# A bidirectional RWKV layer in fp32: the rate and the gate behind the keys, two products on GpSimd, and the output projection's tiles

## The chip, the cores and the metric

One core of a Trainium2 chip runs the whole kernel. The metric is the device time of one execution in microseconds. Of the engines, TensorE (PE, with its weight loads PEld) multiplies matrices; VectorE (DVE), ScalarE (ACT) and GpSimd (POOL) work on elements; SyncE (SP) issues the DMAs. Each engine takes its instructions in the order of its queue, and semaphores hold an instruction until what it needs is there.

## The reference

A model of three mixers over 512 tokens of 1024 channels with 256 context tokens, all in fp32. Layer 0 is pooling and neighbourhood attention with an MLP, layer 1 the recurrence below with an MLP, and a second block has latent and dilated attention. The change lies in layer 1. Its features, cut to what matters:

```python
mix = lambda j: h + centred_shift(h) * mu[j]
k = mix(2) @ wk;  v = mix(3) @ wv                       # keys, values
kk = heads(k * k_k); kk = kk * rsqrt(sum(kk * kk))      # normalised key
for d in range(2):                                      # both directions
    w_raw = w0[d] + tanh(mix(1) @ w1[d]) @ w2[d]        # decay
    a = sigmoid(a0[d] + (mix(4) @ a1[d]) @ a2[d])       # rate
    k_d = k * (1 + (a - 1) * k_a)
r = mix(0) @ wr
g = sigmoid(mix(5) @ g1) @ g2                           # gate
# for each of 16 heads of 64 channels, per token, forward and backward:
S = S * w - (S @ kk) (x) (kk * a) + v (x) k_d;   y = S @ r
# at the end: ((group_norm(y) * ln_g + ln_b + (r . k_sum . r_k) * v) * g) @ wo
```

## The kernel before

The kernel keeps activations as [128 channels, tokens] tiles, 768 columns for context and tokens together. Dense products are made of three fp32r matmuls: weights and activations are split into a high and a low part (`wsplit` L583/L584, `split_sb` L596/L597), and `mm3` (L590 to L592) adds high times high, low times high and high times low.

The framework gives every engine a fixed queue before the run: a planner simulates the program, and among instructions that could go it takes those first that stand earlier in the program. A dependence can be added by hand without a semaphore: `scan.interleave(work, steps)` spreads a list of matmuls over a list of steps, so that each stands behind its step in PE's queue.

**`features`** (L1325) makes the inputs of the recurrence and stores them in DRAM, in this order: the first halves of decay and rate (`lora`, L1382/L1383); the decay's second half, `lora2("w2bd", ...)` into `sd`; the gate's first half; the rate's second half, `lora2("a2bd", ts[1], hw[:,1], self.td, False)`; `mix(2)`, the keys' input (L1369, L596, L597, eight pieces of 128 channels); the gate's second half `gates(tg)` into `gd`; then `proj(wk, ...)`, which makes the keys in units of 256 channels and calls `evac_k` for each block of 128 (copy L1482, square, key norm with a reciprocal square root at L608, reversal for the backward direction, DMAs into `b0` and `b1`); then the same for receptance (`wr`) and values (`wv`). `lora2` has six matmuls for each of 16 heads, a Tanh evacuation of 512 and of 256 columns (L1405) and a store of 393 KB; `gates` has three matmuls, a copy and a store for each of eight blocks. The evacuated tiles of both, and those of `evac_k`, share three tags of two buffers each.

**The scan** (`Scan`) runs over eight blocks of two heads. `front` loads a head's features, makes the running decay (ACT exponentials), turns the rate into `f0` and `ta` (ACT, L368/L369), multiplies these by the normalised key and the key (`base0`, `base1`: L370/L371, VectorE), makes `bk` (L376/L377), `G` (L387/L390) and the products for the bonus (`prod`, L394/L395), then on PE the products in a chunk (L329) that fill `Ld`. `rest` inverts a 32x32 triangle per chunk: mask on GpSimd (L421), transpose on VectorE (L422), thirty steps of two small operations on GpSimd (`Mt` L427, `M` L428), a memset (L429), transposes on VectorE (L432/L433), copies and matmuls into `T` and `f` (L443 to L471); then twelve steps in order over the chunks (L501 to L512, with `ZU` as the state), the sum `Y` (L520), and the normalisation with gate and bonus (L524 to L547), which stores a row block of `z`. `front` of the next block goes beside `rest` of this one as far as the queues let it.

**`layer1`** (L1251) runs the eight blocks and then multiplies `z` by `wo` (1024 x 1024). The 96 matmuls over row blocks 0 to 5 of `z` (L1290) are issued as `work` beside the last block; the first 48 of them are free and the last 48 are pinned over the 23 steps of that block. Their results go to `yp`; the last two row blocks (`wl`, `z[:, 0]` and `z[:, 1]`, L1308) are multiplied and added once the last block is done. The four `wo` tiles are in slots of the third buffer set of the scan (`hp[2]`, which blocks 2 and 5 use), `zl` has a pool of its own, `wl` is loaded again for the last two.

Of the kernel before, what the change touches and what calls it, by code (L numbers as in the profile page):

```python
# [10 lines left out]
F32 = mybir.dt.float32  # L11
# [4 lines left out]
ALU = mybir.AluOpType  # L16
# [4 lines left out]
NX, NC_, D = 512, 256, 1024  # L21
# [3 lines left out]
CH = 64  # L25
# [207 lines left out]
class Scan:  # L233
# [69 lines left out]
    def front(self, blk):  # L303

        nc = self.nc
# [42 lines left out]
        for hd in range(2):  # L348
            h = blk * 2 + hd

            def load(name, n, src):
                t = fp.tile([128, n], F32, name=name, tag=name)
                nc.sync.dma_start(t, src[h])
                return t

            base0, base1, rd = load("base0", NT, self.p.b0), load("base1", NT, self.p.b1), load("rdup", NX, self.p.rd)

            s, ta = load("sg", NT, self.p.sd), load("ta", NT, self.p.td)
            cs = fp.tile([128, NT], F32, name="cs", tag="cs")
            v3 = lambda t: t.rearrange("p (c t) -> p c t", t=CH)  # L360
            nc.vector.tensor_tensor_scan(cs, self.mreset, s, 0.0, ALU.mult, ALU.add)

            for d in range(2):
                nc.scalar.activation(P[dr[d], d, :, 1:], v3(cs)[dr[d]], AF.Exp, scale=-C0)
                nc.vector.tensor_copy(PC[dr[d], hd, :], P[dr[d], d, :, CH])
            nc.scalar.activation(cs, cs, AF.Exp, scale=C0)
            f0 = fp.tile([128, NT], F32, name="f0", tag="sg")
            nc.scalar.activation(f0, ta, AF.Identity, scale=al[:, 0, h:h + 1], bias=be[:, 0, h:h + 1])  # L368
            nc.scalar.activation(ta, ta, AF.Identity, scale=al[:, 1, h:h + 1], bias=be[:, 1, h:h + 1])  # L369
            nc.vector.tensor_tensor(f0, f0, base0, ALU.mult)  # L370
            nc.vector.tensor_tensor(ta, ta, base1, ALU.mult)  # L371
            bk = []
            for g in range(3):
                t = fp.tile([128, 4, 2, CH], F32, name="bk", tag="bk", bufs=4)
                gs = slice(g * 4, g * 4 + 4)
                nc.vector.tensor_tensor(t[:, :, 0, :], v3(f0)[:, gs], v3(cs)[:, gs], ALU.mult)  # L376
                nc.vector.tensor_tensor(t[:, :, 1, :], v3(ta)[:, gs], v3(cs)[:, gs], ALU.mult)  # L377
                bk.append(t)

            Gs = []
            for g in range(3):
                G = self.hp[blk % 3].tile([128, 8 if g else 4, 4, CH], F32, name="G", tag=f"G{g > 0}", bufs=4 if g else 2)
                gs = slice(g * 256, (g + 1) * 256)
                for d, kk in enumerate((base0, base1)):
                    nc.vector.tensor_tensor(G[:, d], v3(kk[:, gs]), P[:, d, g * 4:(g + 1) * 4, :CH], ALU.mult)  # L387
                if g:
                    r = v3(rd[:, (g - 1) * 256:g * 256]).unsqueeze(1).to_broadcast([128, 2, 4, CH])
                    nc.vector.tensor_tensor(G[:, 2:4], r, P[:, :, g * 4:(g + 1) * 4, 1:], ALU.mult)  # L390
                Gs.append(G)

            pr = fp.tile([128, NX], F32, name="prod", tag="cs")
            nc.vector.tensor_tensor(pr[0:64, :], rd[0:64, :], ta[0:64, NC_:], ALU.mult)  # L394
            nc.vector.tensor_tensor(pr[64:128, :][:, ::-1], rd[64:128, :], f0[64:128, NC_:], ALU.mult)  # L395
            bon = self.p.pt("a")
            vr = slice(hd * 64, hd * 64 + 64)
            nc.tensor.matmul(bon[vr, :], self.p.col("rk", h).to_broadcast([128, 64]), pr, start=True, stop=True)
            nc.scalar.copy(vb[vr, :], bon[vr, :])
            heads.append(Gs)  # L400
            for g in range(4):
                if g < 3:
                    products(g, hd, Gs, bk)
                if g:
                    turn(g - 1, Gs, bk)
# [144 lines left out]
class Prog:  # L550
# [700 lines left out]
    def layer1(self, bcs):  # L1251
        tc, nc = self.tc, self.nc
        dt = lambda n, shape: self.dram.tile(shape, F32, name=n)

        self.b0, self.b1 = dt("b0", [16, 128, NT]), dt("b1", [16, 128, NT])
        self.rd, self.vd = dt("rd", [16, 128, NX]), dt("vd", [D, NX])
        self.vt = dt("vt", [2, NT, D])
        self.zd, self.gd, self.bd = dt("zd", [D, NX]), dt("gd", [D, NX]), dt("bd", [D, NX])

        self.sd, self.td = dt("sd", [16, 128, NT]), dt("td", [16, 128, NT])  # L1260
        xd = dt("xd", [128, 8, NX])
        scan = self.features(self.make_cols(1, self.col("ng", 32, 8), 1, 0, True), bcs, xd)
        scan.late()
        scan.rest()
        for blk in range(1, 7):
            scan.front(blk)
            scan.rest()
        scan.front(7)


        early = 6
        zl = scan.pool("l1z", 1).tile([128, early, NX], F32, name="zl")
        w = [scan.hp[2].tile([128, 8, 4, CH], F32, name="wo", tag="GTrue", bufs=4).rearrange("p a c t -> p (a c t)") for u in range(4)]
        for u in range(4):
            nc.sync.dma_start(w[u], self.i["wo"][u])
        for k in range(early):
            nc.sync.dma_start(zl[:, k, :], self.zd[k * 128:(k + 1) * 128, :])
        scan.drop(scan.fp)
        wop = tc.alloc_tile_pool(name="l1w", bufs=1, side="right")
        z, yp = wop.tile([128, 2, NX], F32, name="z"), wop.tile([128, 8, NX], F32, name="yp")  # L1280
        wl = wop.tile([128, 4, 512], F32, name="wl")
        nc.sync.dma_start(wl, self.i["wo"][:, :, early * 256:].rearrange("u p c -> p u c"))
        scan.rest(z[:, 1, :])
        work = []
        for m in range(8):
            for n in range(2):
                ps, o = self.pt("a"), slice(n * 256, n * 256 + 256)
                for k in range(early):
                    c = k * 256 + m % 2 * 128
                    bi = nc.tensor.matmul(ps[:, :256], w[m // 2][:, c:c + 128], zl[:, k, o], start=k == 0, stop=k == early - 1)  # L1290
                    work.append(bi.ins)
                nc.scalar.copy(yp[:, m, o], ps[:, :256])
        nc.sync.dma_start(z[:, 0, :], self.zd[6 * 128:7 * 128, :])
        scan.interleave(work[48:], scan.steps)
        scan.release("left")
        self.psum(mm=4, s0=1, s1=1, s2=1, b=1)
        self.adatag = "b"
        self.xp = tc.alloc_tile_pool(name="xp", bufs=1)
        self.x = self.xp.tile([128, 8, NX], F32, name="x")
        nc.sync.dma_start(self.x, xd)  # L1300
        y = self.y = self.xp.tile([128, 8, NX], F32, name="y")
        gr = (("x", 0, NX, 0),)
        for g, _, n, o in self.halves(gr):
            for m in range(8):
                ps = self.pt("mm")
                for k in range(2):
                    c = k * 256 + m % 2 * 128
                    nc.tensor.matmul(ps[:, :n], wl[:, m // 2, c:c + 128], z[:, k, o:o + n], start=k == 0, stop=k == 1)  # L1308
                nc.vector.tensor_tensor(y[:, m, o:o + n], ps[:, :n], yp[:, m, o:o + n], ALU.add)
        wop.release()  # L1310
        scan.release("right")
        self.wpools(self.wctx)
        with ExitStack() as ctx:
            E = ctx.enter_context
            self.norms()
            act = E(tc.tile_pool(name="l1act", bufs=1))
            h = self.mid(1, None, y, act, gr)
            self.tap("y1", y)
            self.side = self.ada_vec("ada2", "adab2", self.silu[:, 2:3, :].rearrange("p v k -> p k v"), range(24), self.mod[2])
            bcs = self.mlp(1, h, y, gr)  # L1320
            self.bp.release()
        self.tap("x1", self.x)
        return bcs

    def features(self, A1, bcs, xd):  # L1325
        tc, nc = self.tc, self.nc
# [83 lines left out]
        hw = lp.tile([128, 2, 16], F32, name="hw")  # L1410
# [18 lines left out]
        ts = []  # L1429
        for (_, _, func), ps in zip(both_lora, pss):  # L1430
            t = p2.tile([128, NT], F32, name="lr", tag="rev")
# [7 lines left out]
        nc.scalar.activation(t[:, :NX], ps, AF.Tanh, scale=0.5)  # L1439
        nc.vector.tensor_scalar(t[:, :NX], t[:, :NX], 0.5, 0.5, ALU.mult, ALU.add)  # L1440
        tg = split(t, NX)
        lora2("a2bd", ts[1], hw[:, 1], self.td, False)
        first = lambda j, wname, groups: (self.wsplit(self.i[wname][0]), mix(j, groups))
        wk = first(2, "wk", both)
        gates(tg)

        def rev(src, n, b, fwd, bwd):

# [46 lines left out]
            rev(kk, NT, b, self.b0, self.b1)  # L1495

        proj(wk, "wk", both, evac_k)

        def evac_r(b, pss):
            t = p2.tile([128, NT], F32, name="rblk", tag="kblk")  # L1500
# [456 lines left out]
```

## Time and profile before

| | us |
|---|---|
| median of 3 runs (lowest to highest) | 3165.51 (3158.48 to 3166.71) |
| profiled execution, its own time | 3160.86 |
| span of that execution in the profile | 3158.9 |
| busy in the span: PE, VectorE, ACT, GpSimd | 2820.4, 1789.2, 1551.0, 1140.5 |
| moved by DMA | 346.72 MB, 110 GB/s |

The profile is of one execution, so times of the trace go with 3160.86, not with the median. Times in the trace count from the start of the span. Layer 1's features lie at about 1000 to 1263 us, its scan behind them to about 1990. A group's mean is that of one instruction; for matmuls, which overlap in the engine, the pitch from one to the next is shorter than the duration shown. In a row of groups, the part behind the second bar is the idle time ahead of the group and what ended it.

### The profile page before, as it was taken

How to read it: one execution, taken by the hardware profiler on the slowest of the kernel's cores; microseconds unless marked ns; L12 is line 12 of the kernel's file. 1: busy time of each engine (PE TensorE's matmuls, PEld its weight loads, DVE VectorE, ACT ScalarE, POOL GpSimd, SP SyncE). 2: the span in 40 equal slices, each digit the busy share in tenths (PEclk: the TensorE clock that was granted, in tenths of full speed). 3: DMA queues.
4: the chain of work that ended last, by engine and by line, in shares of the span. 5: the costliest groups of instructions: out<-in, count | busy, mean ns of one | idle time of the engine just before them, and what ended most of it. 6: DMA issues, size and time to landing. Idle time of an engine off the chain costs nothing.

```text
span 3158.9 us, 50961 instructions
## 1 busy us (share of the span) xinstructions
PE 2820.4 (89%) x19290; PEld 2338.0 (74%) x19290; DVE 1789.2 (57%) x3558; ACT 1551.0 (49%) x3103; POOL 1140.5 (36%) x1500
## 2 busy tenths in 40 slices
PE   6999879999996899887777779699997999989999
PEld 6967778888885687764666667587776885678887
DVE  8466383444448725758688742644446654555364
ACT  3247556666664633554566532455543444544341
POOL 4013446667665212045666640256543210010000
PEclk9999989999998999987688889899998995999999
DMA  5323213333331465432233231255441220022322
GB/s 225 125 86 101 101 64 117 127 114 131 118 106 72 187 196 149 167 118 84 81 95 106 83 117 50 99 175 183 169 146 54 81 94 1 15 79 90 104 98 83
DMA packets 138115, 346.72 MB, mean 110 GB/s; under 512 B 16400, under 2 KB 48784, under 8 KB 120592
## 3 DMA queue, kind: packets, MB, share of 16 engines
q1 hardware_dynamic: 137872, 343.48, 31.8%
q8 instruction: 152, 2.49, 0.3%
q14 instruction: 91, 0.75, 0.1%
HBM read 294.40 MB, written 49.02 MB: 109 GB/s over the span
## 4 chain that ended last, share of the span: by engine, by line
PE 32%; DVE 8%; ACT 6%; POOL 6%; DMA 4%; issue 2%; SPq 0%; ACTq 0%; POOLq 0%; DVEq 0%
PE mm L590 7%; PE mm L591 7%; PE mm L592 6%; POOL acc L733 3%; DMA adaw<-in_ada_dram 3%; ACT wh L583 1%; PE st L1247 1%; PE a L329 1%; PE a L1290 1%; POOL M L428 1%; POOL Mt L427 1%; PE y L520 1%; ACT adat L732 1%; PE b L1241 1%; PE a L1924 1%
## 5 line engine op out<-in xcount | busy, mean ns | idle before, releaser
L733 POOL TENSOR_TENSOR acc<-acc,adat 128x256 f32<-128x256 f32 x658 | 575.8, 898 | 529.5 <-ACT acc L729 427.7
L584 DVE TENSOR_TENSOR wl<-wr,wh 128x2048 fp32r<-128x2048 f32 (+3 forms) x145 | 317.7, 2191 | 367.1 <-ACT wh L583 364.6
L732 ACT ACTIVATE adat<-adaw,silu 128x256 f32<-128x256 f32 x644 | 319.1, 508 | 262.1 <-POOL acc L733 161.2
L583 ACT CAST wh<-wr 128x2048 fp32r<-128x2048 f32 (+2 forms) x147 | 266.6, 1814 | 232.0 <-PE mm L591 218.1
L590 PE MATMUL mm<-fh,wh 128*128 128x512 f32 (+1 forms) x1008 | 347.3, 353 | 16.1 <-DVE relu L1015 11.7
L591 PE MATMUL mm<-fl,wh 128*128 128x512 f32 (+1 forms) x1008 | 350.8, 350 | 0.0
L592 PE MATMUL mm<-fh,wl 128*128 128x512 f32 (+1 forms) x1008 | 349.8, 349 | 0.9 <-DVE wl L584 0.9
L590 PE MATMUL mm<-h_xhi,wh 128*128 128x512 f32 (+1 forms) x784 | 278.5, 360 | 3.3 <-ACT h_xhi L596 1.9
L591 PE MATMUL mm<-h_xlo,wh 128*128 128x512 f32 (+1 forms) x784 | 277.9, 357 | 1.8 <-DVE h_xlo L686 1.5
L592 PE MATMUL mm<-h_xhi,wl 128*128 128x512 f32 (+1 forms) x784 | 277.8, 356 | 0.0
L664 POOL TENSOR_TENSOR acc<-acc,t 128x256 f32<-128x256 f32 x127 | 109.0, 866 | 345.5 <-ACT t L662 342.6
L590 PEld LDWEIGHTS mm<-fh,wh 128*128 128x128 f32 x1008 | 190.0, 189 | 43.8 <-DVE relu L1015 14.0
L592 PEld LDWEIGHTS mm<-fh,wl 128*128 128x128 f32 x1008 | 190.6, 189 | 25.5 <-DVE wl L584 1.1
L591 PEld LDWEIGHTS mm<-fl,wh 128*128 128x128 f32 x1008 | 190.7, 189 | 25.3 <-DVE fl L597 2.2
L1039 DVE TENSOR_TENSOR y<-mm,y 128x512 f32<-128x512 f32 (+1 forms) x184 | 99.2, 559 | 141.9 <-PE mm L592 141.4
L590 PE MATMUL mm<-h_hi,wh 128*128 128x512 f32 (+1 forms) x408 | 160.8, 398 | 6.7 <-ACT h_hi L685 6.7
L590 PEld LDWEIGHTS mm<-h_xhi,wh 128*128 128x128 f32 x784 | 148.0, 191 | 23.1 <-ACT h_xhi L596 2.1
L592 PEld LDWEIGHTS mm<-h_xhi,wl 128*128 128x128 f32 x784 | 148.9, 190 | 21.4 <-issue 0.2
L591 PEld LDWEIGHTS mm<-h_xlo,wh 128*128 128x128 f32 x784 | 148.9, 191 | 20.7 <-DVE h_xlo L686 1.7
L427 POOL TENSOR_TENSOR Mt<-M 128x30 f32<-128x30 f32 (+14 forms) x240 | 141.0, 588 | 56.3 <-PE f L443 21.8
L591 PE MATMUL mm<-h_lo,wh 128*128 128x512 f32 (+1 forms) x408 | 160.4, 394 | 0.0
L592 PE MATMUL mm<-h_hi,wl 128*128 128x512 f32 (+1 forms) x408 | 159.5, 393 | 0.0
(451 smaller groups left out, 6932.4 us busy)
## 6 DMA issues: line engine op xcount, KB each, us to landing
adaw<-in_ada_dram SPq DMA_DIRECT2D x256, 256.0 KB, 2.7
wr<-in_w_dram SPq DMA_DIRECT2D x64, 1024.0 KB, 4.9
wr<-in_wup_dram SPq DMA_DIRECT2D x22, 1024.0 KB, 4.8
base<-b SPq DMA_DIRECT2D x32, 384.0 KB, 3.2
ZU<-vt SPq DMA_DIRECT2D x192, 64.0 KB, 2.5
wr<-in_wdn_dram SPq DMA_DIRECT2D x16, 704.0 KB, 4.0
wr<-in_win_dram SPq DMA_DIRECT2D x9, 1024.0 KB, 4.7
wr<-in_evin_dram SPq DMA_DIRECT2D x8, 1024.0 KB, 4.8
```

Source lines behind the costliest of these rows:

```text
L329: nc.tensor.matmul(ps[:, c], bk[g][:, c0 + c].rearrange("p a t -> p (a t)"), G[:, :na, c0 + c, :], start=True, stop=True)
L427: nc.gpsimd.tensor_tensor(t, a, b, ALU.mult)
L428: nc.gpsimd.tensor_tensor(M[:, s + 1:, :s], M[:, s + 1:, :s], t, ALU.add)
L583: nc.scalar.copy(hi[:, :n], raw[:, :n])
L584: (eng or nc.vector).tensor_tensor(lo[:, :n], raw[:, :n], hi[:, :n], ALU.subtract)
L590: mm(out, lhs[0], rhs[0], start=first, stop=False)
L591: mm(out, lhs[0], rhs[1], start=False, stop=False)
L592: return mm(out, lhs[1], rhs[0], start=False, stop=last)
L664: nc.gpsimd.tensor_tensor(acc, acc, sq, ALU.add)
L732: nc.scalar.activation(t, w, AF.Copy, scale=s)
L733: nc.gpsimd.tensor_tensor(acc, acc, t, ALU.add)
L1039: nc.vector.tensor_tensor(yb, ps[:, :n], yb, ALU.add)
```

## The change

`lora2("a2bd", ...)` (the rate's second half) and `gates(tg)` (the gate's) move behind `proj(wk, ...)`, ahead of the receptance. In the scan, the two multiplications L370 and L371 go from VectorE to GpSimd. In `layer1`, the third buffer set is released behind block 5 and the feature pool behind the last `front`; one pool then has all of `z` in eight row blocks, `yp` and the four `wo` tiles, which are each loaded once and whole; the reload `wl` goes; the loads of row blocks 0 to 6 of `z` stand behind `rest(7)` in the program; and all 96 matmuls of `work` are pinned over the 23 steps.

```diff
--- before.py
+++ after.py
@@ -367,8 +367,8 @@
             f0 = fp.tile([128, NT], F32, name="f0", tag="sg")
             nc.scalar.activation(f0, ta, AF.Identity, scale=al[:, 0, h:h + 1], bias=be[:, 0, h:h + 1])
             nc.scalar.activation(ta, ta, AF.Identity, scale=al[:, 1, h:h + 1], bias=be[:, 1, h:h + 1])
-            nc.vector.tensor_tensor(f0, f0, base0, ALU.mult)
-            nc.vector.tensor_tensor(ta, ta, base1, ALU.mult)
+            nc.gpsimd.tensor_tensor(f0, f0, base0, ALU.mult)
+            nc.gpsimd.tensor_tensor(ta, ta, base1, ALU.mult)
             bk = []
             for g in range(3):
                 t = fp.tile([128, 4, 2, CH], F32, name="bk", tag="bk", bufs=4)
@@ -1265,33 +1265,30 @@
         for blk in range(1, 7):
             scan.front(blk)
             scan.rest()
+            if blk == 5:
+                scan.drop(scan.hp[2])
         scan.front(7)
-
-
-        early = 6
-        zl = scan.pool("l1z", 1).tile([128, early, NX], F32, name="zl")
-        w = [scan.hp[2].tile([128, 8, 4, CH], F32, name="wo", tag="GTrue", bufs=4).rearrange("p a c t -> p (a c t)") for u in range(4)]
+        scan.drop(scan.fp)
+
+        wop = tc.alloc_tile_pool(name="l1w", bufs=1, side="right")
+        z, yp = wop.tile([128, 8, NX], F32, name="z"), wop.tile([128, 8, NX], F32, name="yp")
+        w = [wop.tile([128, 2048], F32, name=f"wo{u}") for u in range(4)]
         for u in range(4):
             nc.sync.dma_start(w[u], self.i["wo"][u])
-        for k in range(early):
-            nc.sync.dma_start(zl[:, k, :], self.zd[k * 128:(k + 1) * 128, :])
-        scan.drop(scan.fp)
-        wop = tc.alloc_tile_pool(name="l1w", bufs=1, side="right")
-        z, yp = wop.tile([128, 2, NX], F32, name="z"), wop.tile([128, 8, NX], F32, name="yp")
-        wl = wop.tile([128, 4, 512], F32, name="wl")
-        nc.sync.dma_start(wl, self.i["wo"][:, :, early * 256:].rearrange("u p c -> p u c"))
-        scan.rest(z[:, 1, :])
+        scan.rest(z[:, 7, :])
+        early = 6
+        for k in range(7):
+            nc.sync.dma_start(z[:, k, :], self.zd[k * 128:(k + 1) * 128, :])
+        wcol = lambda m, k: w[m // 2][:, k * 256 + m % 2 * 128:k * 256 + m % 2 * 128 + 128]
         work = []
         for m in range(8):
             for n in range(2):
                 ps, o = self.pt("a"), slice(n * 256, n * 256 + 256)
                 for k in range(early):
-                    c = k * 256 + m % 2 * 128
-                    bi = nc.tensor.matmul(ps[:, :256], w[m // 2][:, c:c + 128], zl[:, k, o], start=k == 0, stop=k == early - 1)
+                    bi = nc.tensor.matmul(ps[:, :256], wcol(m, k), z[:, k, o], start=k == 0, stop=k == early - 1)
                     work.append(bi.ins)
                 nc.scalar.copy(yp[:, m, o], ps[:, :256])
-        nc.sync.dma_start(z[:, 0, :], self.zd[6 * 128:7 * 128, :])
-        scan.interleave(work[48:], scan.steps)
+        scan.interleave(work, scan.steps)
         scan.release("left")
         self.psum(mm=4, s0=1, s1=1, s2=1, b=1)
         self.adatag = "b"
@@ -1303,9 +1300,8 @@
         for g, _, n, o in self.halves(gr):
             for m in range(8):
                 ps = self.pt("mm")
-                for k in range(2):
-                    c = k * 256 + m % 2 * 128
-                    nc.tensor.matmul(ps[:, :n], wl[:, m // 2, c:c + 128], z[:, k, o:o + n], start=k == 0, stop=k == 1)
+                for k in range(early, 8):
+                    nc.tensor.matmul(ps[:, :n], wcol(m, k), z[:, k, o:o + n], start=k == early, stop=k == 7)
                 nc.vector.tensor_tensor(y[:, m, o:o + n], ps[:, :n], yp[:, m, o:o + n], ALU.add)
         wop.release()
         scan.release("right")
@@ -1439,10 +1435,8 @@
         nc.scalar.activation(t[:, :NX], ps, AF.Tanh, scale=0.5)
         nc.vector.tensor_scalar(t[:, :NX], t[:, :NX], 0.5, 0.5, ALU.mult, ALU.add)
         tg = split(t, NX)
-        lora2("a2bd", ts[1], hw[:, 1], self.td, False)
         first = lambda j, wname, groups: (self.wsplit(self.i[wname][0]), mix(j, groups))
         wk = first(2, "wk", both)
-        gates(tg)
 
         def rev(src, n, b, fwd, bwd):
 
@@ -1495,6 +1489,8 @@
             rev(kk, NT, b, self.b0, self.b1)
 
         proj(wk, "wk", both, evac_k)
+        lora2("a2bd", ts[1], hw[:, 1], self.td, False)
+        gates(tg)
 
         def evac_r(b, pss):
             t = p2.tile([128, NT], F32, name="rblk", tag="kblk")
```

## Rows read from the trace of the kernel before

**Rows 1.** The page's first part: busy us, share of the span, instructions.

```profile
PE 2820.4 (89%) x19290; PEld 2338.0 (74%) x19290; DVE 1789.2 (57%) x3558; ACT 1551.0 (49%) x3103; POOL 1140.5 (36%) x1500
```

**Rows 2.** Windows: stretch, its us, each engine's busy us (instructions), PEclk, DMA share, GB/s.

```profile
1077.00:1112.00 35.00, 31.52 (x133) 21.65 (x132) 25.03 (x40) 27.96 (x59) 2.68 (x1) 1.00 0.72 264
...
1196.00:1210.00 14.00, 7.70 (x44) 7.48 (x44) 9.05 (x22) 4.67 (x8) 2.10 (x5) 0.79 0.85 254
...
1263.00:1340.00 77.00, 65.65 (x423) 56.64 (x422) 57.49 (x111) 41.13 (x80) 2.17 (x3) 0.91 0.47 162
...
1400.00:1830.00 430.00, 329.68 (x4376) 255.07 (x4373) 335.10 (x719) 246.70 (x594) 250.54 (x393) 0.81 0.28 88
...
1902.00:1975.00 73.00, 71.19 (x736) 55.76 (x738) 19.33 (x68) 16.07 (x42) 1.26 (x1) 0.94 0.15 43
...
1975.00:1991.00 16.00, 4.41 (x38) 3.86 (x36) 9.84 (x17) 5.35 (x5) 1.26 (x1) 0.73 0.72 264
```

**Rows 3.** Timeline of ACT: start, us, engine, line, operation, tiles, [wait and releaser].

```profile
1062.74 12.98 ACT L1405 ACTIVATE lr_out<-mm,hw 128x512 f32<-128x512 f32 x25
...
1127.34 0.37 ACT L1482 COPY kblk<-mm 128x256 f32<-128x256 f32 x1 [12.42 <-PE mm L592]
...
1131.73 1.28 ACT L608 ACT_TABLE_LOAD   x1
```

**Rows 4.** Groups by line on PE, 1077 to 1112: busy us, mean ns of one.

```profile
L590 PE MATMUL mm<-lr_hi,wh 128*128 128x512 f32 (+1 forms) x40 | 17.4, 436 | 3.5 <-ACT wh L583 1.5 <-ACT lr_out L1405 1.4
```

**Rows 5.** Timeline of DVE: first and last of `mix(2)`, the key projection's input.

```profile
1083.30 0.48 DVE L1369 SCALAR_TENSOR_TENSOR mix_t<-xc,cols,hc 128x256 f32<-128x256 f32 x1 [0.73 <-PE mm L1383]
...
1102.73 0.69 DVE L597 TENSOR_TENSOR mixl<-mix_t,mixh 128x512 fp32r<-128x512 f32 x1 [1.04 <-ACT mixh L596]
```

**Rows 6.** Operations of one line: lowest, median, highest ns, first and last start, shapes.

```profile
L370 DVE TENSOR_TENSOR f<-f,base x16: 940/957/1362, 1275.6 to 1783.4; 128x768 f32<-128x768 f32 x16
...
L371 DVE TENSOR_TENSOR ta<-ta,base x16: 940/955/1071, 1279.9 to 1786.1; 128x768 f32<-128x768 f32 x16
...
L421 POOL TENSOR_TENSOR Ld<-Ld,c_mdiag x8: 1793/1801/2297, 1332.5 to 1829.4; 128x768 f32<-128x768 f32 x8
...
L422 DVE STREAM_TRANSPOSE M<-Ld x8: 1918/1952/1982, 1337.5 to 1832.1; 128x1024 f32<-128x1024 f32 x8
...
L429 POOL MEMSET M<- x8: 152/158/158, 1377.4 to 1868.0; 128x32 f32 x8
```

**Rows 7.** The chain that ended last, 1400 to 1830, by line.

```profile
by line: PE a L329 8.8%; issue 6.7%; DVE G L387 5.5%; PE y L520 4.2%; PE a L398 3.8%; PE f L467 3.4%; DVE G L390 3.4%; PE f L453 3.0%; DVE G L332 2.7%; DVE bk L376 2.6%; DVE prod L394 2.5%; PE b L508 2.4%; DVE bk L377 2.4%; DVE ZU L512 2.3%
```

**Rows 8.** Timelines of POOL and DVE: where `M` is done, and who reads it.

```profile
1678.26 0.16 POOL L429 MEMSET M<- 128x32 f32 x1
...
1684.95 1.93 DVE L432 STREAM_TRANSPOSE Ld<-M 128x1024 f32<-128x1024 f32 x1
...
1868.00 0.16 POOL L429 MEMSET M<- 128x32 f32 x1
...
1869.10 1.90 DVE L432 STREAM_TRANSPOSE Ld<-M 128x1024 f32<-128x1024 f32 x1 [13.10 <-POOL M L428]
```

**Rows 9.** Waits, 1400 to 1830: who waits <- for whom, us, times, longest.

```profile
POOL Ld L421 <- ACT Ld L335: 83.3, 6, 28.6
```

**Rows 10.** Groups by line on POOL: 1400 to 1830, then 1832 to 1870.

```profile
L428 POOL TENSOR_TENSOR M<-M,Mt 128x30 f32<-128x30 f32 (+9 forms) x180 | 117.4, 652 | 13.4
...
L428 POOL TENSOR_TENSOR M<-M,Mt 128x30 f32<-128x30 f32 (+14 forms) x30 | 15.5, 515 | 2.3
```

**Rows 11.** The chain that ended last, 1900 to 1991, by line.

```profile
by line: PE a L1290 42.1%; PE y L520 9.3%; DMA rb<-gd 7.1%; DMA rb<-bd 5.8%; PE b L501 5.8%; PE f L467 5.0%; PE b L508 4.0%; DMA zl<-zd 3.0%; PE b L509 2.9%; POOL sq L539 2.8%; PE y L627 2.3%; PE mm L1308 2.1%; issue 2.1%; PE y L530 1.7%; D
```

**Rows 12.** Groups by line on PE: 1845 to 1870, then 1870 to 1991.

```profile
L1290 PE MATMUL a<-zl,wo 128*128 128x256 f32 x30 | 7.8, 396 | 0.5 <-DMA wo<-in_wo_dram 0.5
...
L1290 PE MATMUL a<-zl,wo 128*128 128x256 f32 x162 | 44.1, 412 | 3.5 <-DMA zl<-zd 3.5
```

**Rows 13.** Timeline of SP: the `wo` loads.

```profile
1879.91 0.81 SPq L1275 DMA_DIRECT2D wo<-in_wo_dram  x2
```

## The prediction

> **What bounds the kernel now.** I read the first part of the page, then the windows of the three stretches that the diff touches, then the chain of waits in each, then single rows. The page names TensorE: 2820.4 of 3158.9 us busy, twice ACT's share, with VectorE at 57% and GpSimd at 36% [rows 1]. That is a mean over stages with different limits, and the windows show it [rows 2]. In the features of layer 1, behind 1077, PE is busy 31.5 of 35 us, but at the border between keys and receptance (1196 to 1210) only 7.7 of 14. In the first three heads of the scan (1263 to 1340) VectorE has 57.5 of 77 and GpSimd 2.2. In the body of the scan (1400 to 1830) four engines stand at 58 to 78%, and VectorE, not PE, is the fullest by a little. In the output projection over the last block (1902 to 1975) PE has 71.2 of 73, then 4.4 of 16. So the first part of the change must be read as an order of work on PE, the second as a balance among engines in a stage that no engine bounds, the third as filling.
>
> **Part 1: rate and gate behind the keys.** Nothing is removed; 96 + 24 matmuls and their evacuations move. ACT's row has 25 evacuations of alternately 512 and 256 columns in 12.98 us [rows 3]: 1.04 us a head, which is 3 x 768 columns of PE, so 0.451 ns a column. The rate is 16 x 1.04 = 16.6 us, the gate's 24 matmuls of 512 columns 5.5 us: 22.2 us of PE, and the 40 first-of-three matmuls in 1077 to 1112 are all of them [rows 4]. The keys' first unit (96 matmuls, 36,864 columns, 16.6 us) is evacuated at 1127.34 [rows 3], so it began about 1110.7. Its input, `mix(2)`, is on VectorE from 1083.30 and complete at 1102.73 + 0.69 = 1103.4 [rows 5]. With rate and gate out of the way, the unit follows `mix(2)`: the last of its eight k steps takes 2.1 us, so it ends at 1105.5, 21.8 us earlier. What is late next there is `mix(2)` itself: more than these 21.8 can't be had without a faster VectorE.
>
> Behind the keys the 22.2 us come back, less what they fill. The border has 14 - 7.7 = 6.3 us of idle PE, in which VectorE makes the receptance's input [rows 2]. Filled in full: -21.8 + 22.2 - 6.3 = -5.9. ACT alone would need there its 4.67 us of now, 40 evacuations at 0.52 us (20.8) and two table loads of 1.28 us: 28 us, under PE's 7.7 + 22.2 = 29.9, so PE sets it, narrowly. The 16 + 8 stores on SP (393 KB and 262 KB) move into a stretch with a DMA share of 0.85 [rows 2], where the next weight tiles also load; the rate is first read by the scan at about 1270, so the stores are not late. The evacuated tiles share three tags with those of the keys: the first three heads wait for the last key block's stores, a few us. Upper end: none of the idle filled and the table loads bare, -21.8 + 22.2 + 2.6 = +3. Lower end: the wait for `mix(2)` shrinks too, as VectorE's and ACT's work of rate and gate leaves the stretch, by some 4 us: -10. I take **-6**.
>
> ACT now goes Tanh, then the square root of the key norm (table load at 1131.73, 1.28 us [rows 3]); after, Tanh comes again behind it: two loads more at 1.28 us if the last key block closes first, more if its square root falls between the heads. The Trainium skill, "ScalarE: Activation LUTs", section "Table sets: the hidden batching unit", says that activations of different sets in turn pay for the load each time, which speaks against this change. The row here agrees on the size of one load; no row of this kernel shows such alternation.
>
> **Part 2: two multiplications of each head on GpSimd.** VectorE is rid of 16 x (0.957 + 0.955) = 30.6 us [rows 6]. GpSimd gets 32 operations of that shape; its only one of 128x768 with two inputs, L421, takes 1.80 us [rows 6], so 57.6 us in all, 7.2 us for each of eight blocks. In the first three heads GpSimd is idle and VectorE at 75%: there 3 x 1.9 us go from VectorE and about half of that from the path, -3. In the body (L422 runs eight times from 1337.5 to 1832.1, so blocks of 70.7 us [rows 6]) VectorE's lines G, bk, prod and ZU sum to 21.4 of the 53.7% that the chain's listed lines hold, 40% [rows 7]; bk and prod wait for these products. Each link now is 0.85 us longer in its own duration, while VectorE's queue is 3.8 us shorter a block; 3.8 x 0.40 = -1.5. GpSimd has the recursion of M, sixty small operations in dependence, which take 36 us from L422's start to the memset in the last block and 40 in the first [rows 6, 8]. VectorE reads M at L432 as soon as it is ready: from the start of the closing memset to the start of L432 there are 1.1 to 6.7 us in seven blocks, mean 2.6 [rows 8]. GpSimd is busy 58% of the body; of 7.2 us some 4.2 so fall into the recursion, 1.6 above the mean slack. The rest falls where GpSimd waits for ACT anyway, 83.3 us ahead of L421 [rows 9]. Per block -1.5 + 1.6, with VectorE's shorter queue also handing G to PE earlier, which I put at -0.2: about -0.1, so -1 for seven. With -3: **-4**. Ends: every microsecond of VectorE's on the path, -31; 7 x (7.2 - 2.7), all in the recursion, +31. I stay near the middle because both engines have gaps, and nearer to the gain because GpSimd's gaps are in whole pieces.
>
> L428 takes 652 ns at the mean in the body and 515 in 1832 to 1870, where VectorE is nearly idle [rows 10]: the two slow each other. The Trainium skill, "SBUF — State Buffer", section "Who interferes with whom", says that VectorE and GpSimd share a port pair and that one holds it for a whole instruction. By that rule a 1.8 us multiplication on GpSimd would hold up VectorE's two-input operations too, and the part would give nothing or lose; the rows agree in direction. The rival below is this.
>
> **Part 3: the output projection's early matmuls.** L1290 is 42.1% of the chain in 1900 to 1991, 38 us [rows 11]. Now the first 48 matmuls may run when they can, the other 48 are pinned over the last block's 23 steps; after, all 96 are, and the four `wo` tiles no longer wait for slots of `hp[2]`, whose last two loads go out at 1879.91 [rows 13]. The 15 matmuls (30 records) that now run in an idle stretch by 1870 go behind, +7.8 us [rows 12]. The pause of 3.5 us on `zl` at 1901.7 [rows 12] should go: PE has steps to do until the row lands, -3.5. And PE's last 16 us, with 11.6 idle [rows 2], can take what is left of the backlog as the last block starts sooner, half to two thirds, -7.3. Sum **-3**. Ends: -11 if the idle is filled whole and the 15 stay covered by steps that wait; +7 if nothing fills it and PE waits for the same row as now. SP carries the seven `z` loads behind `rest(7)` in the program, and the `ZU` loads beside them; up to 4 MB of `wo` stand before these, hence the plus side. The removed `wl` load (1 MB) costs no path now.
>
> **Sum.** -6 - 4 - 3 = -13. The profiled execution took 3160.86 us (span 3158.9), the median of the runs is 3165.51, 4.65 more. 3160.9 - 13 = 3147.9 there, so **3152** against the median.
>
> **Rivals.**
> 1. *VectorE bounds the scan.* Its 335 us are the most of the four [rows 2], and G, bk and prod are the chain's VectorE lines [rows 7]. Then part 2 gives nearly all of 30.6, some -29, and with -6 and -3 the time is 3127. Against it: VectorE idles 22% of the body, PE's lines hold more of the chain.
> 2. *GpSimd's chain decides (slower).* The multiplications of the next block's heads sit in GpSimd's queue ahead of or between the links of M. It decides from the point where more than the slack of 1.1 to 6.7 us [rows 8] of the 7.2 falls into the recursion: 7 x (7.2 - 2.7) = +31, with -6 and -3 that is +22: 3187. For it: GpSimd's 652 against 515 ns; against it: the waits of 83 us ahead of L421.
> 3. *Nothing is left.* The border becomes ACT's with table loads among heads (-1), part 2 is even (0), and all fillers end before the last step with the 15 behind (+4): +3, 3168. For it: the margins of ACT against PE at the border (28 to 30 us) and of VectorE against GpSimd are thin.
>
> **How the numbers follow.** A measurement of this kernel can tell about 0.3%, 9.5 us, from no change. The forecast has 0.42, with its own range of 3138 to 3162; rival 1 has 0.13, rival 2 0.20, rival 3 0.25. Faster by over 9.5 us (under 3156): most of the forecast (0.36) and rival 1, 0.49. Slower (over 3175): rival 2 and a bit of rival 3, 0.23. Between: 0.28. The range goes from inside rival 1 (3122) to rival 2's price (3187).
>
> **What would show it.** Part 1: first copy of a key block near 1105 rather than 1127, and the first receptance matmul some 6 us earlier than now; a border of over 36 us, or more than three table loads there, makes it wrong. Part 2: the starts of L422 closer than 70 us apart; if L432 starts right behind the memset of M in every block and the pitch grows, rival 2. Part 3: no pause on a `z` row, PE over half busy in the 16 us behind the last L1290. Wrong altogether: a scan's body that moves by more than 15 us either way.

## The result, and the profile after

The changed kernel takes 3207.23 us (median of 4 runs, 3204.6 to 3211.27) against 3163.17 (4 runs) of the kernel before: ratio 1.0133, 95% interval 1.0116 to 1.0151. That is 44 us slower by the medians, 42 by the ratio. The forecast was 13 us faster; the time lies above its range.

The page's first part after, in the same columns as [rows 1]: GpSimd has 45 us more and PE 27 more for the same number of matmuls. VectorE has 31 instructions less, two multiplications of each head among them, and yet no less busy time: its other operations became longer by about what it was rid of.

```profile
PE 2847.0 (89%) x19290; PEld 2362.7 (74%) x19290; DVE 1790.7 (56%) x3527; ACT 1552.1 (48%) x3104; POOL 1185.7 (37%) x1532
```

The windows after, placed on the same work as [rows 2]: the making of `mix(2)`, the border with rate and gate in it, the first heads, the body, the output projection and the readout behind it.

```profile
1077.00:1107.00 30.00, 27.86 (x131) 20.38 (x131) 23.35 (x40) 16.22 (x31) 6.48 (x6) 1.00 0.35 130
...
1174.00:1215.00 41.00, 33.97 (x165) 27.93 (x164) 23.90 (x44) 31.93 (x58) 5.04 (x9) 0.88 0.80 274
...
1263.00:1349.00 86.00, 71.70 (x464) 62.09 (x464) 64.48 (x115) 42.99 (x84) 13.98 (x10) 0.90 0.45 149
1400.00:1868.00 468.00, 352.57 (x4498) 275.49 (x4500) 343.45 (x714) 248.01 (x609) 283.29 (x418) 0.77 0.26 82
...
1943.00:2016.00 73.00, 71.87 (x820) 57.93 (x820) 21.17 (x75) 17.19 (x44) 1.27 (x1) 1.00 0.16 47
2016.00:2032.00 16.00, 6.54 (x44) 5.47 (x42) 8.16 (x16) 5.38 (x5) 2.60 (x1) 0.70 0.62 230
```

Laid over the trace of before, with the start of layer 1's features (984.4 and 989.9) set to zero in both, the changed kernel is ahead by 27.2 us at the last key block; level at the last receptance block; 3.5 late at the first transpose of M (L422); 30.8 late at the last; 41.7 late at the start of the last recursion, 43.4 at its end; 37.9 late at the last sum of the output projection. The other 9 us of the two spans lie in code that is the same in both, 5.5 of them ahead of the features. Sixteen profiles of changed kernels have the features begin at 984.5 to 993.1, fourteen of them at 989.5 or later, so the profiled execution of before was a quick one, and those 9 us are not the change's.

The scan's rows that answer to [rows 6]: L371 now stands on POOL at 1.87 us; L422 runs from 1346.5 to 1868.3, seven pitches of 74.5 us in place of 70.7.

```profile
L371 POOL TENSOR_TENSOR ta<-ta,base x16: 1802/1872/2190, 1282.9 to 1823.2; 128x768 f32<-128x768 f32 x16
...
L422 DVE STREAM_TRANSPOSE M<-Ld x8: 1930/1958/1983, 1346.5 to 1868.3; 128x1024 f32<-128x1024 f32 x8
```

POOL's timeline in block 3 shows where the products went. The links of the recursion follow each other in dependence, and L370 and L371 stand between two of them:

```profile
1591.49 0.33 POOL L427 TENSOR_TENSOR Mt<-M 128x84 f32<-128x84 f32 x1
1591.90 0.35 POOL L428 TENSOR_TENSOR M<-M,Mt 128x84 f32<-128x84 f32 x1
1592.26 2.00 POOL L370 TENSOR_TENSOR f<-f,base 128x768 f32<-128x768 f32 x1
1594.21 0.37 POOL L427 TENSOR_TENSOR Mt<-M 128x108 f32<-128x108 f32 x1
1594.54 1.99 POOL L371 TENSOR_TENSOR ta<-ta,base 128x768 f32<-128x768 f32 x1
1596.49 0.58 POOL L428 TENSOR_TENSOR M<-M,Mt 128x108 f32<-128x108 f32 x1
```

And its end in the last block, with the transpose behind it, the counterpart of [rows 8]: the memset L429 is not the end of the recursion. Three links stand behind it in the queue, and in the kernel before they stood there too.

```profile
1916.83 0.16 POOL L429 MEMSET M<- 128x32 f32 x1
1916.97 0.29 POOL L428 TENSOR_TENSOR M<-M,Mt 128x58 f32<-128x58 f32 x1
1917.35 0.23 POOL L427 TENSOR_TENSOR Mt<-M 128x30 f32<-128x30 f32 x1
1917.66 0.25 POOL L428 TENSOR_TENSOR M<-M,Mt 128x30 f32<-128x30 f32 x1
...
1919.10 1.90 DVE L432 STREAM_TRANSPOSE Ld<-M 128x1024 f32<-128x1024 f32 x1
```

### The profile page after: what moved, and what is told of

Read it like the earlier page. It is cut to its first block, busy times and chain, and to the rows that moved or that the text cites. A ratio compares the mean times of both kernels' runs of the same rounds, so it can differ in the third digit from the quotient of the medians.

```text
span 3206.0 us, 51053 instructions
## 1 busy us (share of the span) xinstructions
PE 2847.0 (89%) x19290; PEld 2362.7 (74%) x19290; DVE 1790.7 (56%) x3527; ACT 1552.1 (48%) x3104; POOL 1185.7 (37%) x1532
## 5 line engine op out<-in xcount | busy, mean ns | idle before, releaser
L592 PEld LDWEIGHTS mm<-fh,wl 128*128 128x128 f32 x1008 | 192.0, 191 | 26.2 <-DVE wl L584 1.3
L427 POOL TENSOR_TENSOR Mt<-M 128x30 f32<-128x30 f32 (+14 forms) x240 | 134.4, 560 | 95.7 <-PE f L443 48.8
```

The source lines that it names most:

```text
L427: nc.gpsimd.tensor_tensor(t, a, b, ALU.mult)
L592: return mm(out, lhs[1], rhs[0], start=False, stop=last)
```

## Experiments

Differences in us are the ratio to the kernel before, run on the same chip, less one, times its median there (3167.6 to 3171.0). "The base" is the kernel with first and third part alone. A trace is of one execution, and not always of a typical one, so a difference between two traces can lie some 10 us off the difference in time.

**Each part alone, and two without the third.**

> The kernel before with the two multiplications of each head on GpSimd, nothing else. Theory L (a loop through one scratch slot decides the scan): the recursion's scratch Mt and the transposed Dd share one slot, so block b+1's recursion on GpSimd starts only when the matmuls L443 have read block b's Dd; GpSimd's multiplications fall between the links, the loop of 70.7 us grows to 74 to 77 us in seven blocks, and the run is 25 to 45 us slower than before. Rival P (the lengthening is in each head's own path, 1.8 instead of 0.96 us twice): 16 x 1.7 = 27 us at most, also seen with the recursion's blocks no closer to their f matmuls. Rival K (the loss comes from the order of all three parts together): this part alone within 10 us of before.

> The kernel before with rate and gate behind the keys, nothing else. Theory: the keys come some 26 us earlier, the border gives all of it back, as it took 28 us more in the changed kernel, so the time is within 6 us of before. Rival (the scan's first heads start 3 us later because of the late rate): 3 to 8 us slower. The prediction's own figure: 6 us faster.

> The kernel before with the new tiles and the pinning of all 96 early matmuls, nothing else. Theory: 8 us faster, as in the changed kernel the distance from the last recursion to the readout shrank by 6 to 8 us. Rival (that gain exists only because the last block came late there, the z rows being in memory long before): 0 to 3 us faster.

> The changed kernel with the multiplications of each head back on VectorE (first and third part kept). Theory: 0 to 10 us faster than before, so the second part alone is worth 40 to 50 us. Rival K (the three parts act together): still 15 us or more slower than before.

```diff
 # e1: only this of the change        # e4 (the base): all but this
-nc.vector.tensor_tensor(f0, f0, base0, ALU.mult)
-nc.vector.tensor_tensor(ta, ta, base1, ALU.mult)
+nc.gpsimd.tensor_tensor(f0, f0, base0, ALU.mult)
+nc.gpsimd.tensor_tensor(ta, ta, base1, ALU.mult)
 # e2: only the two lines moved behind proj(wk, ...);  e3: only layer1
```

| | ratio | 95% | us |
|---|---|---|---|
| second part alone | 1.0152 | 1.0138 to 1.0165 | +48 |
| first part alone | 0.9983 | 0.9972 to 0.9995 | -5 |
| third part alone | 1.0035 | 1.0022 to 1.0048 | +11 |
| first and third (the base) | 1.0015 | 1.0006 to 1.0024 | +5 |

The second part is the loss, whichever other parts stand beside it: 48 alone, a little over theory L's 45, 44 - 5 = 39 on the base (37 by the ratios). The first part gives what the prediction said. The third costs 11 alone and 10 on top of the first; my theory of a gain there was wrong.

**Is it the loop through the one slot of `Mt` and `Dd`?**

> The changed kernel with a slot of its own for Dd, so that block b+1's recursion no longer waits for the matmuls L443 of block b. Theory L (the loop recursion, transposes, L443, next recursion decides the body): five of seven blocks waited 6 to 11 us there, so 25 to 45 us faster than the changed kernel, 0 to 20 slower than before. Rival P (each head's own path through the slower products decides): under 10 us faster than the changed kernel, 35 or more slower than before.

> First and third part, multiplications on VectorE, and a slot of its own for Dd. Theory L: the loop sets the pace here too, but with waits of 11, 2, 3 and 3 us only, so 5 to 20 us faster than the same without the slot, that is 0 to 15 faster than before. Rival (without GpSimd's multiplications the loop is covered by VectorE and PE): within 4 us of the same without the slot.

```diff
-        Dd = sp.tile([128, 32, 32], F32, name="Dd", tag="Mt")
+        Dd = sp.tile([128, 32, 32], F32, name="Dd", tag="Dd")
```

On the changed kernel 1.0122 (1.0099 to 1.0146), 39 us slower than before: 3 to 5 better, inside the two intervals, where the theory wanted 25 to 45. The loop through L443 exists, but it is not what the products lengthen. The time is the one that rival P gave; the next runs test its cause. On the base the slot gives what was expected: 0.9963 (0.9949 to 0.9978), 12 us faster than before, 16 better than the base.

**GpSimd's time, VectorE's time, and the consumers apart.**

> First and third part; VectorE multiplies as before, and GpSimd makes both products once more into a scratch tile that nobody reads. It prices GpSimd's 57.6 us without a consumer and without relief for VectorE. Theory L: they fall between the recursion's links all the same, 30 to 50 us slower than before. Rival P (the loss is that bk and prod wait for a slower producer): under 10 us slower than before.

> First and third part, and the multiplications left out: f0 and ta are made by ACT from base0 and base1 in place of the rate, so the products with the rate are not computed. It prices VectorE's 30.6 us alone. Theory L (VectorE is in the loop only at its two transposes): 3 to 12 us faster than the same with them, about 5 faster than before. Rival D (VectorE bounds the scan, the prediction's first rival): 25 to 31 us faster than before.

> First and third part, multiplications on VectorE; GpSimd makes in each head two more operations of 128x768 on a tile of its own that reads only this head's decays and that nothing waits for. It prices GpSimd's time alone, without a consumer, a tile slot or relief for VectorE. Theory O (occupancy: what falls between two links of the recursion lengthens it one for one): some 20 of the 32 fall there, 35 us, so 25 to 40 us slower than the same without, 30 to 45 slower than before. Rival F (the loss is in the fronts of the heads, which wait for the products in GpSimd's queue): under 10 us slower than the same without.

```diff
 # e7, ahead of VectorE's own two:
+dum = fp.tile([128, NT], F32, name="dum", tag="dum")
+nc.gpsimd.tensor_tensor(dum, f0, base0, ALU.mult)
+nc.gpsimd.tensor_tensor(dum, ta, base1, ALU.mult)
 # e8, VectorE's two left out:
+nc.scalar.activation(f0, base0, AF.Identity, scale=al[:, 0, h:h + 1])
+nc.scalar.activation(ta, base1, AF.Identity, scale=al[:, 1, h:h + 1])
 # e9, behind VectorE's two; self.dum is one tile for the whole scan:
+for _ in range(2):
+    nc.gpsimd.tensor_tensor(self.dum, self.dum, PC[:, hd, 0:1].to_broadcast([128, NT]), ALU.mult)
```

The e7 products cost 55 us against before (1.0173, 1.0151 to 1.0195), more than theory L's 30 to 50. But VectorE writes `f0` and `ta` in place behind them and so waits for them; that run doesn't free the consumers. The e9 run does, and costs as much: 1.0169 (1.0155 to 1.0182), +54, 49 above the base, more than the 25 to 40 expected. So the consumers of rival P are not needed for the loss. Its rows (L375 is the added operation, L426 the transpose L422 of before):

```profile
L375 POOL TENSOR_TENSOR dum<-dum,PC x32: 1457/1644/2237, 1281.5 to 1844.2; 128x768 f32<-128x768 f32 x32
...
L426 DVE STREAM_TRANSPOSE M<-Ld x8: 1900/1950/1997, 1347.4 to 1889.8; 128x1024 f32<-128x1024 f32 x8
```

From the first to the last transpose 542.4 us; the base has 498.7 (1339.3 to 1838.0). So two added operations per head on GpSimd make the loss, even when nothing waits for them. Summed over the timeline, the eight recursions, each from its first to its last link, take 353.5 us in the base, 391.7 in the changed kernel and 406.8 here. Of the added operations 34.7 us (changed kernel) and 32.8 (here) lie inside, and GpSimd also stands idle ahead of some of them inside, 8.8 and 16.6 us, because the operation waits for ACT or for the head's decays and the next link stands behind it. The seven gaps between one recursion's last link and the next one's first sum to 182.8, 177.7 and 175.4 us. So all of the lengthening lies inside the recursions, and none in the gaps, which hold VectorE's transposes, L443 and the rest of the next front. The changed kernel's waits on POOL, 1400 to 1880 (who <- for whom: us, times, longest):

```profile
POOL f L370 <- ACT f L368: 16.7, 3, 10.1
...
POOL f L370 <- DMA base<-b: 4.0, 2, 3.7
```

The relief of VectorE (e8): 0.9943 (0.9929 to 0.9958), 18 faster than before and 23 better than the base, so by time between the two theories. In the trace only 3 of it are there by the end of layer 1's attention and 15 arise in the second block, whose code is the same and whose data are not. For the scan I take the 3.

**Dose, place and the other engine.**

> First and third part; GpSimd multiplies in heads 0 to 2 alone, where it has nothing else, VectorE in the other thirteen. The prediction's step for these heads: 3 us faster than the same without. Theory F: the first transpose of M comes 4 to 8 us later as each product takes 0.85 us longer and bk waits for it, and nothing else changes: 0 to 8 us slower than the same without, 5 to 13 slower than before. Theory O: 0 to 3 us either way.

> First and third part; one of the two multiplications of each head (ta by base1) on GpSimd, the other on VectorE: half the dose, with consumers. Theory O (GpSimd's time between the links decides): about half of the 39 us that both cost, 15 to 25 us slower than the same without, 18 to 32 slower than before. Rival Q (any operation of the fronts on GpSimd upsets the order of the queues, however little work it is): 30 or more slower than the same without, or none.

> First and third part; the two idle operations per head of 128x768 that GpSimd had are given to VectorE instead, on top of its own: 30 us more for VectorE, which the windows show as the fullest engine. Theory O (VectorE has room, GpSimd's chain has not): under 15 us slower than the same without. Rival D (VectorE is as tight as GpSimd): 25 or more slower.

```diff
 # e10
+(nc.gpsimd if h < 3 else nc.vector).tensor_tensor(f0, f0, base0, ALU.mult)   # and ta
 # e13: ta alone on GpSimd
+nc.gpsimd.tensor_tensor(ta, ta, base1, ALU.mult)
 # e14: the loop of e9 on VectorE
+nc.vector.tensor_tensor(self.dum, self.dum, PC[:, hd, 0:1].to_broadcast([128, NT]), ALU.mult)
```

Half the dose: 1.0070 (1.0049 to 1.0092), +22, so 17 above the base against 39 for both. (Its recursions take 378.7 us, 25 more than the base's against 38 for both; that trace is of the slowest of four executions.) The same idle operations on VectorE, 30.7 us in all: 1.0028 (1.0013 to 1.0042), +9, 4 above the base against 49 on GpSimd. In its trace, of the quickest of ten executions, they make 4 us by the end of the last recursion and 14 by the last sum of the output projection; e9 has 54 and 55 there. VectorE has room and GpSimd's recursion has not, though VectorE is the busier of the two in the profile; its window (1342 to 1847) shows it at 396 of 505 us:

```profile
1342.00:1847.00 505.00, 374.49 (x4813) 294.18 (x4811) 396.35 (x800) 272.76 (x647) 303.09 (x462) 0.81 0.28 89
```

The three heads alone: 1.0053 (1.0038 to 1.0068), 12 above the base, more than any theory gave. 7 of them are there at the first transpose, as expected. In the trace another 14 arise in the body, 512.8 against 498.7 us, which is more than the time shows in all:

```profile
L422 DVE STREAM_TRANSPOSE M<-Ld x8: 1937/1947/1978, 1346.1 to 1858.9; 128x1024 f32<-128x1024 f32 x8
```

No operation of the body differs, but the planner ordered all five queues anew. In the other kernels whose scan has the same operations this stretch has 494.6 to 502.8 us, so a new order, with one execution's chance, may be worth some 8 us; that it makes all 14 here isn't shown.

**The tail, and better versions.**

> First and third part with the first 48 early matmuls free again, so that only the new tiles are left of the third. If the pins cost the 7.8 us of matmuls that ran early before: 5 to 10 us faster than with all 96 pinned, 2 to 5 faster than before. If the tiles themselves cost it (wo and z loaded later): no faster than with all pinned.

> The same as the one before it with a slot of its own for Dd, multiplications on VectorE: the version that the runs so far point to. Theory: 10 to 20 us faster than before. Rival: the slot's gain needs the pins, then as fast as with pins, about 11 us faster than before, or less.

> First and third part (48 matmuls free), a slot of its own for Dd, and the reverse of the second part: the mask L421, the product L539 and the memset L488 go from GpSimd to VectorE, 26 us off GpSimd, about 16 of them between links or as idle time ahead of them. Theory O: 5 to 15 us faster than the version without this, 16 to 26 faster than before. Rival D: slower than the version without this, as VectorE has 15 us more.

```diff
 # e11, and in e12 with the slot for Dd
-        scan.interleave(work, scan.steps)
+        scan.interleave(work[48:], scan.steps)
 # e15 = e12 and
-nc.gpsimd.tensor_tensor(Ld[:, :24, :32], ...)   # also vb * g (L539) and the memset L488
+nc.vector.tensor_tensor(Ld[:, :24, :32], ...)
```

Free pins alone: 1.0022 (1.0011 to 1.0033), +7, no better than all 96 pinned. With the slot: 0.9966 (0.9954 to 0.9978), 11 faster than before, the same as with pins. The pins are not what the third part costs. What is left of it is the tiles, with the loads and the order that follow from them; which of these costs the time isn't shown. The reverse of the second part: 0.9970 (0.9957 to 0.9983), 10 faster than before, no gain on e12, which neither theory gave. Its recursions take 322.8 us in all, 27 less than in e12, and the body is no shorter (L422 from 1338.4 to 1845.9, against 1338.7 to 1834.9): the gaps between the recursions grew by 39. So in these runs the price is one-sided: time put between the links shows nearly in full, time taken out did not, though here VectorE also had 15 us more. Of the versions run that compute the whole layer, first and third part with the slot is the fastest, by a margin over e12 and e15, 1 to 2 us, that is inside the noise. The first part with the slot and without the third, whose price of 10 us would then go, was not run.

## Why the prediction was wrong

**First part: -6 forecast, -5 timed, both halves larger.** The keys' first block is evacuated at 1106.5 (5.5 of that the late start) rather than 1127.3, 26.2 earlier; 21.8 was the term. `mix(2)` itself ended 2.8 us sooner, the case I had named for the lower end, and the first copy follows its last piece by 0.5 us, not by the 2.1 of a whole k step. The border then took back 27 and not 15.9. The step that failed is "filled in full", with "PE sets it, narrowly". In the 41 us PE is busy 34.0, where I had 29.9, at a mean granted clock of 0.88; and it is idle for 7.0, where I had nothing. Half of that, 3.4 us, is for ACT's evacuations, ahead of the same group of 40 as in [rows 4]; ACT has 31.9 us there, since the receptance's casts and weight splits, most of which I left out of ACT's 28, fall in too. The other half, 3.5, is what was left of the waits of the key norm for VectorE's `rb`, which I had as filled:

```profile
L590 PE MATMUL mm<-lr_hi,wh 128*128 128x512 f32 (+1 forms) x40 | 16.1, 403 | 3.5 <-ACT lr_out L1401 3.4
...
PE st L627 <- DVE rb L623: 3.5, 2, 1.9
```

The table loads fell among the heads, three in 6 us (L1401 is the Tanh, L608 the square root):

```profile
1183.24 1.28 ACT L1401 ACT_TABLE_LOAD   x1 [3.12 <-DVE kkblk L1487]
1185.60 1.28 ACT L608 ACT_TABLE_LOAD   x1
1187.54 1.28 ACT L1401 ACT_TABLE_LOAD   x1 [0.43 <-DMA b<-kkblk]
```

Tanh, root, Tanh pay 3.8 us. That is what the Trainium skill says in "ScalarE: Activation LUTs", section "Table sets: the hidden batching unit": each change of set pays a load, and the trace agrees. Of the figures in its section "What ACT_TABLE_LOAD costs" the trace shows the load, 1.28 us, but not the 1.38 us of drain added to each: 5.6 us hold three loads and three activations. At most about a third of the 11 us that the border took beyond the forecast is theirs. So gain and border cancel in the trace (level at the last receptance block), and in e2's own trace the last sum is level with before too. The -5 in time is not placed, and that it agrees with -6 is luck.

**Second part: -4 forecast, 37 to 48 more.** Three steps failed.

*The slack.* "...from the start of the closing memset to the start of L432 there are 1.1 to 6.7 us in seven blocks, mean 2.6." The memset does not close anything: it writes the diagonal, which no link touches, and the planner set it ahead of the last three links. From the last link to L432 the kernel before has 0.0, 0.0, 0.0, 0.5, 5.6, 0.7, 1.7 and 0.0 us, mean 1.1, with none in four of the eight blocks. The row itself had said so: the last one in [rows 8] ends with "[13.10 <-POOL M L428]", a wait of 13 us of VectorE for the recursion.

*What falls inside.* That 4.2 of 7.2 us a block fall into the recursion was right: 34.7 of the 61.1 us that the products took, 57%. That GpSimd's other waits take up the rest was right too: the gaps between the recursions did not grow. But the forecast set a slack against those 4.2 us, and it had no term for a product that itself waits inside the recursion (8.8 us). The recursions became 38 us longer, and no later wait gave any of it back. Why the gaps keep their length, so that a late recursion makes the next one late in full, is open; the e5 run shows that the wait for L443 is not the reason. The sign that I had named for rival 2 came only by half: the pitch grew, but L432 starts 3.0 us behind the last link at the mean, so VectorE, too, comes late to it.

*The gain on VectorE.* -1.5 a block, from 40% of the chain, would be 10 us for the body; the trace of e8 gives 3 for the whole scan. A share of the chain of waits is not a price. The same 40% of the row is VectorE in e14, and 30 us more of VectorE cost 4. Nor was the relief there to be had, as VectorE's busy time did not fall. In the first heads, -3 forecast, the transpose came 7.5 later than in the base (356.7 against 349.1 from the start of the features). GpSimd was idle there, and the products and their readers stand one behind the other, so I put this down to the longer duration of each.

Rival 2 had mechanism and sign; its +31, worked out with the wrong slack, was too small. Without a slack, what lies inside the recursions, 34.7 and 8.8, is 43 us, near the 37 to 48 measured. PE's granted clock was lower as well: a mean of 0.82 in the body of the base and of 0.78 in that of the changed kernel, both mixtures of the two levels, 1.2 and 2.4 GHz. PE is busy 394 us there for some 4800 matmuls, where the base has 377. Whether this adds to the loss or only goes with it isn't shown.

```profile
1339.00:1838.00 499.00, 376.86 (x4849) 292.33 (x4850) 371.01 (x778) 271.94 (x646) 280.83 (x462) 0.82 0.29 91
...
1346.00:1868.00 522.00, 394.28 (x4806) 308.08 (x4808) 367.81 (x754) 268.21 (x642) 321.17 (x488) 0.78 0.28 89
```

The other rule that I had weighed, the Trainium skill's "SBUF — State Buffer", section "Who interferes with whom", is borne out for VectorE. Beside the two products of block 3 shown in the result (1592.26 to 1594.26 and 1594.54 to 1596.53), VectorE's timeline (DVE, 1590 to 1597) has

```profile
1592.82 1.47 DVE L365 COPY PC<-P 64x12 f32<-64x12 f32 x1
...
1594.90 0.29 DVE L332 TENSOR_TENSOR G<-a,c_mscan 64x128 f32<-64x128 f32 x1
1595.22 1.59 DVE L376 TENSOR_TENSOR bk<-f,cs 128x256 f32<-128x256 f32 x1
```

The copy has a median of 0.20 us in the body and `bk` of 0.43; here each ends 0.03 and 0.28 us behind the product beside it. `L332`, which reads PSUM, keeps its 0.29. Summed over the body, VectorE's operations that overlap one of over 1.3 us on GpSimd took some 25 us more than the same lines elsewhere, against 5 in the base; that is where most of VectorE's relief went. It does not account for the loss: the gaps did not grow, and the links of the recursion on GpSimd became shorter, 609 ns at the mean against 652 in [rows 10].

```profile
L428 POOL TENSOR_TENSOR M<-M,Mt 128x30 f32<-128x30 f32 (+9 forms) x180 | 109.6, 609 | 12.7
```

**Third part: -3 forecast, about +10.** The pause on `z` did not go, and the idle end was hardly filled. The early matmuls wait 4.4 us for a row of `z` (3.5 in [rows 12]):

```profile
L1288 PE MATMUL a<-z,wo 128*128 128x256 f32 x192 | 50.3, 404 | 4.4 <-DMA z<-zd 4.4
```

PE has 6.5 busy of the 16 us behind the steps (4.4 before), so 2 and not 7.3 were filled. All 192 records now lie there, and the last steps come every 5.6 us rather than 3.7. The sum by the forecast's own terms, +7.8 + 0.9 - 2.1, is +7, its upper end; the 11 measured lie some 4 above that. But the pins, which these terms price, are not confirmed as the cause, since freeing 48 gave nothing. Nor do the traces place the loss in this stage. From the end of the last recursion to the last sum the kernel before takes 138.8 us, the changed one 133.3, the base 133.2, and the third part alone 141.7. At that sum the base is 3 us ahead of before and the third part alone 8 behind, though by time they are 5 and 11 slower. The code behind, the same in all, takes 1137 to 1162 us in the seventeen profiles. So the filling failed as read, and the cause of the third part's price stays open.

## What to carry to other kernels

An engine at 58% that carries a serial chain may have no room inside the chain: price work given to it by what falls between two links, and by the idle time that it brings there, not by the engine's idle share. Read the end of a chain from the releaser that the consumer's row names, not from the last line of the source. Test a suspected engine with idle work on it: here the same two operations cost 49 us on the emptier engine and 4 on the fuller one. And don't count on relief of one engine as a gain: in e8 hardly any of it showed in the scan, and in e15 none.

## What the runs showed of the hardware that was not expected

A multiplication of 128x768 with one operand broadcast from a column took 1.64 us on GpSimd (median of 32), with two full operands 1.87 (16, same stage). A copy of 64x12 on VectorE (L365), 0.17 us at the median of 32 in the changed kernel, took 1.15 to 1.70 in the seven cases in which it began within one of the two products on GpSimd, and each time it ended 0.03 us behind that. So the products took from VectorE's other work about what they had taken off it. Yet on this stage the order on GpSimd's queue was the larger effect.
